# Attention scores as two row tiles of three products, with keys and queries kept in place

## The chip, the cores and the metric

The kernel runs on one core of one Trainium2 chip. The time is the device time of one execution in microseconds; the lower the better. A matmul here is one instruction of TensorE with its own weight load; VectorE, ScalarE and GpSimd each run their instructions in order, and SyncE (SP) issues all DMAs from one queue in order.

## The reference, cut to what matters

The program is a two-layer trunk over 1024 latent and 256 context tokens: differential attention, a dense MLP, an S5 mixer with a GLU, and a second MLP, with norms and gates between. Only the attention is touched by the change. There are 8 heads; each has two softmax maps over the same values:

```python
def attend(q, k, v):
    s = jnp.einsum('bqhcd,bkhcd->bhcqk', q, k).astype(jnp.float32)   # c = 2 maps, d = 64
    p = jax.nn.softmax(s, axis=-1)
    w = p[:, :, 0] - lam * p[:, :, 1]
    o = jnp.einsum('bhqk,bkhe->bqhe', w.astype(v.dtype), v)          # e = 128
    return rmsnorm(o, subln_g) * (1.0 - lambda_init)
```

Latent queries read all 1280 keys, context queries the 256 context keys. Queries and keys of latent tokens are rotated by their position before this. All operands are float32.

## The kernel before

**Precision.** A float32 operand x is kept as two fp32r numbers, hi (x rounded) and lo (x - hi). Most products are made as three: hi x hi, hi x lo and lo x hi (`mm3`, lines 130 to 134).

**Units.** The attention (`phase_b`, line 679) runs over 8 heads of 9 units each, 72 in all. Unit 0 holds two tiles of 128 context queries against 256 keys; units 1 to 8 hold one tile of 128 latent queries each against 1280 keys. Two units (1 and 2, 3 and 4, ...) are a pair of 256 queries. The instructions of the four compute engines are written in a fixed order by hand (`manual`, line 644); a framework puts in the waits between engines.

**One unit, in the order written** (loop at line 876):

- `scores` (568): both maps of the unit into PSUM. The two maps' 64 features have hi and lo stacked to 128 rows. For each map the keys are one array of [hi; lo], and the queries are there twice, as [hi; lo] and as [lo; hi], so that two products over 128 rows make all four terms. A unit of 1280 keys takes 8 products of 512 columns and 4 of 256. Map 0 fills columns 0 to 1280 of PSUM (banks 0, 1 and half of 2), map 1 columns 1280 to 2560 (the other half of bank 2, banks 3 and 4).
- `maxima` (584, L594): one VectorE pass per map copies scores out of PSUM and takes the row's minimum of the negated scores.
- `values` (713), in units where a pair is complete: 30 products of 256 columns of the weights `wT` with the values of the head, into bank 6.
- Three parts, each with transpositions of the *previous* unit's weights (`w_part`, L627: 4, 2 and 4 blocks of 128 keys), then a fill: some of the eight projection products (three matmuls each) of one group of the *next* head's keys or queries. The table AHEAD says which unit projects which group: units 0, 2, 5 and 7 have a group of 512 tokens, 1 and 3 one of 256, units 4, 6 and 8 none. FILLS says how the eight are cut over the parts, (0, 3, 6, 8) if nothing else is given.
- Part 0 is read out by ScalarE (hi, L635) and VectorE (lo, L636); parts 1 and 2 by a ScalarE copy (L640) and two GpSimd passes (L641, L642). Parts 0 and 2 of a unit with a group share bank 5; without a group part 2 uses bank 7, which the projections use otherwise. Part 1 uses half of bank 6.
- Between them stand, for this unit, the first exponential (`exps`, L604 on ScalarE) in part 0, and in part 1 the second exponential and `combine` (L612, L613, L615 on VectorE: w = p0 - factor x p1). In units with `values` of a latent pair ("late"), parts 0 and 1 are read out only behind `combine`.
- At the end: the pair's output (`pair_out`, L724, L725), its row sums one unit later (`pair_sums`, L731), and pieces of the projection's own tail (`next_post`): read-out (L528, L529, or L523, L524 for context), a swap of rows by four DMAs, a GpSimd product (L534), an addition (L537) and the hi/lo split (`split`, L137 on ScalarE and L138 on VectorE).

**Keys and queries by way of DRAM.** The split of a group goes into a staging buffer, and two DMAs store it to `Kd` or `Qd`. The next head's keys are loaded again as one array per map (`load_k`), the queries by three DMAs for each pair of tiles (`load_q`). The last of these loads are issued behind unit 8's scores.

**Beside it.** Unit 3 also holds three small VectorE instructions of the previous head's norm (L737 to L739); head 7 has no projections, but 60 products of the output projection in parts of six (`wo_group`).

Of the kernel before, what the change touches and what calls it, by code (L numbers as in the profile page):

```python
# [13 lines left out]
KB = 256  # L14
# [56 lines left out]
class Prog:  # L71
# [431 lines left out]
    def proj_group(self, h, T, g, wt):  # L503
# [7 lines left out]
        q, sw, qc, s = self.rq, self.rs, self.rc, self.stg[:, :, 0:n]  # L511
# [4 lines left out]
        def out():  # L516
            dst = self.Kd if T else self.Qd
            for c in range(2):
                self.dma(dst[h % 2, c, :, c0 : c0 + n].rearrange("(l r) n -> r l n", l=2),
                         s[64 * c : 64 * c + 64].bitcast(F32))  # L520

        def direct():
            nc.scalar.activation(s[:, 0], b, AF.Copy, scale=scale)  # L523
            nc.vector.scalar_tensor_tensor(s[:, 1], b, scale, s[:, 0].bitcast(F32), ALU.mult, ALU.subtract)  # L524
            out()
# [13 lines left out]
        def store():  # L539
            self.split(s[:, 0], s[:, 1], qc)  # L540
            out()
# [25 lines left out]

    def scores(self, u, Q, K):
        mm = self.nc.tensor.matmul
        if u == 0:  # L570
            for t in range(2):
                for c in range(2):
                    o = self.PS[:, 512 * t + 256 * c : 512 * t + 256 * c + 256]
                    for r in range(2):
                        mm(o, Q[:, c, r, 128 * t : 128 * t + 128], K[c][:, 0:256], start=r == 0, stop=r == 1)
            return
        qs = slice(128 * ((u - 1) % 2), 128 * ((u - 1) % 2) + 128)
        for c in range(2):
            for k0, k1 in (((0, 512), (512, 1024), (1024, 1280)), ((0, 256), (256, 768), (768, 1280)))[c]:
                for r in range(2):  # L580
                    mm(self.PS[:, 1280 * c + k0 : 1280 * c + k1], Q[:, c, r, qs], K[c][:, k0:k1], start=r == 0, stop=r == 1)  # L581


    def maxima(self, u, p, sm):
        ts = self.nc.vector.tensor_scalar
        if u == 0:
            for t in range(2):
                for c in range(2):
                    i = 512 * t + 256 * c
                    ts(p[c][:, 256 * t : 256 * t + 256], self.PS[:, i : i + 256], 1.0, None, ALU.mult, ALU.min,  # L590
                       accum_out=sm[:, 2 * t + c : 2 * t + c + 1])
        else:
            for c in range(2):
                ts(p[c], self.PS[:, 1280 * c : 1280 * c + 1280], 1.0, None, ALU.mult, ALU.min, accum_out=sm[:, c : c + 1])  # L594
# [21 lines left out]

    def w_part(self, u, w, n, tb):

        if u == 0:
            for kt in range(2):  # L620
                for t in range(2):
                    self.nc.tensor.transpose(tb[:, 256 * kt + 128 * t : 256 * kt + 128 * t + 128],
                                             w[:, 256 * t + 128 * kt : 256 * t + 128 * kt + 128], self.ident)
            return shaped(tb, (2, 256)), self.wT[0][:, 0:2], self.wT[1][:, 0:2]
# [1954 lines left out]
```

## Time and profile before

| | us |
|---|---|
| median of 3 runs | 2850.67 (2849.14 to 2854.11) |
| the profiled execution, its span | 2849.8 |
| head 0, first scores to the next head's | 222.7 to 293.5 |
| heads 1 to 6 | 293.5 to 763.5 |
| head 7 and what follows it in this stage | 763.5 to about 870 |

The profiled execution has no other time than its span; it lies within the three runs, and their median is 0.9 us above it. Rows of a timeline give the start in us from the span's start, the duration, engine, line, operation, what it writes and reads and its shape; brackets hold the idle time of the engine before it and what ended that. Rows of stretches give, for each engine, the time in which it was busy and its instructions. A duration on TensorE reaches to the end of the pipeline; how fast products follow each other is seen from their starts.

### The profile page before, as it was taken

The page shows a single profiled execution, that of the slowest core. Times are in us where ns is not written, and L with a number is a line of the kernel's source. Part 1 is how long each engine was busy: PE and PEld are TensorE (multiplying, and loading weights), DVE is VectorE, ACT ScalarE, POOL GpSimd, SP SyncE. Part 2 cuts the span into 40 slices and gives each one's busy share as a digit, 9 for nine tenths or more (in the row PEclk, how much of TensorE's full clock was granted, in tenths as well). Part 3 has the DMA queues.
Part 4 walks back from the last instruction along what each step waited for, and adds up shares of the span by engine and source line. Part 5 has one row for each costly group of instructions (what it writes and reads, how often), then busy time and mean ns, then how long its engine had stood idle before and what let it go on. Part 6 is the DMA issues. An engine that isn't in the chain of part 4 may idle for free.

```text
span 2849.8 us, 43385 instructions
## 1 busy us (share of the span) xinstructions
PE 2723.3 (96%) x15229; PEld 2283.1 (80%) x15229; DVE 2019.8 (71%) x2984; ACT 1369.5 (48%) x2583; POOL 1037.2 (36%) x901
## 2 busy tenths in 40 slices
PE   6999999999999999999999999789999999999999
PEld 4688888888877887778877878688887778888887
DVE  6357788888873667767698878799543597668466
ACT  3425555565653753333444445487444633344443
POOL 3314676766663600000030013688121143336414
PEclk9999999999999999999999999899999999999999
DMA  9955555655825359886799878579742144476544
GB/s 279 319 172 188 152 173 172 177 171 171 256 91 182 128 179 316 294 302 216 249 312 310 272 238 263 169 228 306 235 154 98 66 163 160 155 246 227 167 131 142
DMA packets 414823, 586.30 MB, mean 206 GB/s; under 512 B 41870, under 2 KB 260236, under 8 KB 411404
## 3 DMA queue, kind: packets, MB, share of 16 engines
q1 hardware_dynamic: 414604, 583.52, 63.5%
q8 instruction: 120, 1.97, 0.3%
q14 instruction: 99, 0.81, 0.1%
HBM read 396.38 MB, written 182.82 MB: 203 GB/s over the span
## 4 chain that ended last, share of the span: by engine, by line
PE 76%; DVE 9%; DMA 5%; issue 4%; POOL 3%; ACT 2%; SPq 1%; DVEq 0%; ACTq 0%; POOLq 0%
PE PS L132 21%; PE PS L134 20%; PE PS L133 20%; PE PS L581 4%; PE PS L627 2%; PE PS L1928 2%; PE PS L1963 2%; DMA FU<-in_mlp_w 1%; DMA Ta<-FU 1%; PE PS L202 1%; DVE R L138 1%; SPq L80 1%; DVE F L615 1%; ACT F L604 1%; DVE H L138 1%
## 5 line engine op out<-in xcount | busy, mean ns | idle before, releaser
L132 PE MATMUL PS<-H 128*128 128x512 f32 x1072 | 420.6, 393 | 2.7 <-ACT H L137 1.7
L134 PE MATMUL PS<-H 128*128 128x512 f32 x1072 | 417.5, 390 | 2.8 <-DVE H L138 1.5
L133 PE MATMUL PS<-H 128*128 128x512 f32 x1072 | 417.7, 390 | 0.0
L132 PE MATMUL PS<-H,R 128*128 128x512 f32 (+1 forms) x828 | 308.0, 374 | 4.3 <-ACT R L137 2.0
L133 PE MATMUL PS<-H,R 128*128 128x512 f32 (+1 forms) x828 | 298.6, 361 | 0.0
L134 PE MATMUL PS<-H,R 128*128 128x512 f32 (+1 forms) x828 | 298.0, 361 | 0.0
L132 PEld LDWEIGHTS PS<-H 128*128 128x128 f32 x1072 | 201.2, 188 | 50.5 <-issue 6.4
L134 PEld LDWEIGHTS PS<-H 128*128 128x128 f32 x1072 | 201.2, 188 | 46.1 <-DVE H L138 2.3
L133 PEld LDWEIGHTS PS<-H 128*128 128x128 f32 x1072 | 201.3, 188 | 40.6
L604 ACT ACTIVATE F<-F,stat 128x1280 f32<-128x1280 f32 x128 | 174.3, 1362 | 106.6 <-DVE F L594 106.5
L137 ACT ACTIVATE H<-U 128x640 fp32r<-128x640 f32 x216 | 131.9, 674 | 172.6 <-PE PS L133 138.3
L137 ACT ACTIVATE R<-W 128x512 fp32r<-128x512 f32 (+1 forms) x184 | 128.7, 707 | 174.1 <-PE PS L133 101.5
L132 PE MATMUL PS<-R,H 128*128 128x512 f32 x520 | 208.0, 401 | 3.3 <-ACT H L137 3.3
L134 PE MATMUL PS<-R,H 128*128 128x512 f32 x520 | 205.0, 396 | 1.8 <-DVE H L138 1.8
L133 PE MATMUL PS<-R,H 128*128 128x512 f32 x520 | 204.5, 394 | 0.0
L138 DVE TENSOR_TENSOR H<-U,H 128x640 fp32r<-128x640 f32 x216 | 165.1, 797 | 50.6 <-ACT H L137 49.6
L138 DVE TENSOR_TENSOR H<-W,H 128x512 fp32r<-128x512 f32 (+1 forms) x137 | 125.2, 924 | 102.8 <-ACT H L137 102.1
L594 DVE TENSOR_SCALAR_CACHE_REDUCE F<-PS 128x1280 f32<-128x1280 f32 x128 | 185.2, 1483 | 9.3 <-PE PS L581 9.1
L137 ACT ACTIVATE H<-W 128x512 fp32r<-128x512 f32 (+2 forms) x158 | 95.4, 613 | 188.7 <-PE PS L133 116.8
L132 PEld LDWEIGHTS PS<-H,R 128*128 128x128 f32 x828 | 157.6, 191 | 30.2 <-issue 4.1
L134 PEld LDWEIGHTS PS<-H,R 128*128 128x128 f32 x828 | 157.0, 190 | 25.2 <-issue 0.8
L641 POOL TENSOR_SCALAR R<-F 128x256 fp32r<-128x256 f32 (+1 forms) x128 | 126.5, 989 | 136.0 <-ACT F L640 122.4
(534 smaller groups left out, 6860.0 us busy)
## 6 DMA issues: line engine op xcount, KB each, us to landing
W<-in_mlp_w SPq DMA_DIRECT2D x176, 256.0 KB
U<-Aa SPq DMA_DIRECT2D x108, 320.0 KB
Aa<-FU SPq DMA_DIRECT2D x91, 320.0 KB
Ad<-F SPq DMA_DIRECT2D x112, 256.0 KB
W<-Ad SPq DMA_DIRECT2D x112, 256.0 KB
FU<-in_mlp_w SPq DMA_DIRECT2D x32, 512.0 KB
Ta<-FU SPq DMA_DIRECT2D x16, 1024.0 KB
U<-in_ada_w SPq DMA_DIRECT2D x32, 512.0 KB
```

The costliest lines, as they stand in the source:

```text
L132: mm(out, ah, bh, start=first, stop=False, **kw)
L133: mm(out, ah, bl, start=False, stop=False, **kw)
L134: mm(out, al, bh, start=False, stop=last, **kw)
L137: self.nc.scalar.activation(hi, src, AF.Copy)
L138: (lo_eng or self.nc.vector).tensor_tensor(lo, src, hi.bitcast(F32), ALU.subtract)
L581: mm(self.PS[:, 1280 * c + k0 : 1280 * c + k1], Q[:, c, r, qs], K[c][:, k0:k1], start=r == 0, stop=r == 1)
L594: ts(p[c], self.PS[:, 1280 * c : 1280 * c + 1280], 1.0, None, ALU.mult, ALU.min, accum_out=sm[:, c : c + 1])
L604: nc.scalar.activation(p[c], p[c], AF.Exp, bias=sm[:, c : c + 1], scale=-1.0, accum_out=sn[:, 0:1] if c else s0[:, u + 1 : u + 2])
L627: self.nc.tensor.transpose(tb[:, 128 * (kt - k0) : 128 * (kt - k0) + 128], w[:, 128 * kt : 128 * kt + 128], self.ident)
L641: nc.gpsimd.tensor_scalar(hi, t, 1.0, 0.0, ALU.mult, ALU.add)
L1928: mm(b[:, o : o + 160], X[:, d, i, 64 * j : 64 * j + 128], U[:, 4 * n + i, cols], start=True, stop=True)
L1963: mm(o, cs[d][n % 2][j][:, i], W[:, d, i], start=False, stop=d == 1 and j == 1)
```

## The change

1. **Scores.** Hi and lo are no longer stacked. Keys and queries are each two arrays, hi and lo, of 128 rows: map 0 in rows 0 to 63, map 1 in rows 64 to 127. For each chunk of keys there are three products (hi x hi, hi x lo, lo x hi) for each map, over 64 rows, the two maps in turn. Map 0 and map 1 use different rows of TensorE and different PSUM banks: map 0 columns 0 to 1280, map 1 columns 1536 to 2816. The term lo x lo is no longer computed. A unit of 1280 keys has 18 products in place of 12.
2. **In place.** For heads 1 to 7 the split writes keys and queries straight into the arrays that the scores read: two sets of keys, for even and odd heads, and one set of queries. Only head 0 still goes by way of `Kd` and `Qd`. The buffer R1 grows by 5 KB per partition to hold this.
3. **Banks of the transpositions.** In units with a group, part 0 goes to the unused halves of banks 2 and 5, as part 2 does in all units; part 0 of a unit without a group goes to bank 7.
4. **Order.** The first fill stands before part 0, the second before part 2, the third behind it. With the new FILLS the third is empty but in unit 1. The first exponential and the pair's sums stand ahead of part 0, the pair's output ahead of `combine`.

```diff
-    FILLS = {1: (0, 0, 4, 8), 3: (0, 4, 8, 8)}
+    FILLS = {0: (0, 4, 8, 8), 1: (0, 0, 4, 8), 2: (0, 3, 8, 8), 3: (0, 7, 8, 8)}
...
-        q, sw, qc, s = self.rq, self.rs, self.rc, self.stg[:, :, 0:n]
+        q, sw, qc = self.rq, self.rs, self.rc
+        hi, lo = (self.stg[:, j, 0:n] for j in range(2)) if h == 0 else self.operand(h, T, g)
...
         def store():
-            self.split(s[:, 0], s[:, 1], qc)
+            self.split(hi, lo, qc)
             out()
...
     def scores(self, u, Q, K):
...
+        if u == 0:
+            todo = [(256 * t, 256, 0, 128 * t) for t in range(2)]
+        else:
+            todo = [(k0, n, k0, 128 * ((u - 1) % 2)) for k0, n in ((0, 512), (512, 512), (1024, 256))]
+        for o, n, k0, q0 in todo:
+            for i, (x, y) in enumerate(((0, 0), (0, 1), (1, 0))):
                 for c in range(2):
...
+                    r = slice(64 * c, 64 * c + 64)
+                    self.nc.tensor.matmul(self.PS[:, 1536 * c + o : 1536 * c + o + n], Q[x][r, q0 : q0 + 128],
+                                          K[y][r, k0 : k0 + n], start=i == 0, stop=i == 2)
...
+    def part_bank(self, i):
+        b = self.PS
+        if i == 7:
+            return bass.AP(b.tensor, b.offset + 512 * 7, [list(b.ap[0]), [256, 2], [1, 256]])
+        return bass.AP(b.tensor, b.offset + 1280, [list(b.ap[0]), [1536, 2], [1, 256]])
...
-        Kr = Ring([self.view(self.R1, 5 * i, (1280,)) for i in range(3)])
...
+        Ks = [[self.view(self.R1, 10 * i + 5 * j, (1280,)) for j in range(2)] for i in range(2)]
...
+        qhi = self.view(self.R1, 20, (1280,))
+        Qs = [[qhi[:, 256:768], qhi[:, 768:1280], qhi[:, 0:256]], [self.rv(12, 512), self.rv(14, 512), self.rv(56, 256)]]
...
-                    a = self.FILLS.get(u, (0, 3, 6, 8))
+                    a = self.FILLS.get(u, (0, 4, 8, 8))
...
+                def part(i):
+                    if i < parts:
+                        tb = pb[:, 256:512] if i == 1 else self.part_bank(7 if i == 0 and not groups else 2)
+                        ready.append((*self.w_part(prev[1], prev[2], i, tb), i == 0))
+
                 if pv:
                     values(*pv)
...
+                fill(0)
+                if front:
+                    self.exps(u, 0, p, sm, s0, sn)
...
+                while sums and sums[0][0] <= n:
+                    sums.pop(0)[1]()
+                part(0)
+                if not late:
                     next_post()
+                    evac()
+                part(1)
+                if late:
+                    next_post()
+                if front:
+                    self.exps(u, 1, p, sm, s0, sn)
                 if pv:
                     pair_out(*pv)
...
+                    self.combine(u, p, s0, sn)
+                evac()
+                fill(1)
+                part(2)
+                evac()
+                fill(2)
+                if front and u == 0:
+                    next_post()
                 next_post()
```

More of the change, by code (lines that the diff above doesn't have):

```diff
@@ L894, in phase_b @@
                         load_v(h + 1)
[L895 to L897 removed]
                     if h < 7:
                         groups = [self.proj_group(h + 1, *a, wts[a[0]]) for a in (self.AHEAD[u],)] if u in self.AHEAD else []
[L900 to L904 removed]
+                    self.scores(u, queries(pair), Ks[h % 2])
                     self.maxima(u, p, sm)
```

133 lines of the change are left out of this document (47 added, 86 removed).

## The prediction

> **What bounds the kernel now.** I read the page's span and its chain of waits first, then the table by stretch for one attention head, then who waited for whom from 300 to 760 us, then the timelines of three engines through that head.
>
> ```profile
> span 2849.8 us, 43385 instructions
> ...
> PE 76%; DVE 9%; DMA 5%; issue 4%; POOL 3%; ACT 2%; SPq 1%; DVEq 0%; ACTq 0%; POOLq 0%
> ```
>
> ```profile
> 528.59:558.89 30.30, 27.93 (x175) 24.59 (x174) 24.58 (x44) 17.86 (x42) 19.10 (x20) 1.00 0.80 239
> 558.89:583.52 24.63, 23.43 (x155) 20.75 (x153) 20.92 (x33) 14.85 (x28) 18.23 (x18) 1.00 0.52 148
> 583.52:606.93 23.41, 23.41 (x157) 21.21 (x155) 20.14 (x27) 14.07 (x26) 15.98 (x15) 1.00 0.37 104
> sum 78.34, PE 74.77 PEld 66.56 DVE 65.64 ACT 46.78 POOL 53.32; mean PE 24.92 PEld 22.19 DVE 21.88 ACT 15.59 POOL 17.77
> ```
>
> ```profile
> DVE stat L612 <- ACT F L604: 50.4, 41, 2.0
> ```
>
> The three stretches are head 4: units 0 to 2, 3 to 5, 6 to 8. TensorE looks like the bound, 74.77 of 78.34 us. But VectorE has 65.64 us of work, and much of its idle time cannot be filled: its largest wait is for an exponential, 1.2 us at a time. Each unit has a loop through the engines: scores (TensorE), two row minima (L594, VectorE), two exponentials (L604, ScalarE), the combination (L612, L613, L615, VectorE). VectorE works in order, so the next unit's minima stand behind this unit's combination. Its rows in units 3 to 5:
>
> ```profile
> 558.85 1.09 DVE L138 TENSOR_TENSOR R<-FC,R 128x512 fp32r<-128x512 f32 x1
> 560.05 0.69 DVE L529 SCALAR_TENSOR_TENSOR FC<-PS,W 128x512 f32<-128x512 f32 x1
> 560.66 1.48 DVE L594 TENSOR_SCALAR_CACHE_REDUCE F<-PS 128x1280 f32<-128x1280 f32 x1
> ...
> 562.06 1.49 DVE L594 TENSOR_SCALAR_CACHE_REDUCE F<-PS 128x1280 f32<-128x1280 f32 x1
> ...
> 565.44 0.16 DVE L612 RECIPROCAL stat<-stat 128x1 f32<-128x1 f32 x1 [1.28 <-ACT F L604]
> ...
> 569.26 1.48 DVE L594 TENSOR_SCALAR_CACHE_REDUCE F<-PS 128x1280 f32<-128x1280 f32 x1
> ...
> 573.68 0.16 DVE L612 RECIPROCAL stat<-stat 128x1 f32<-128x1 f32 x1 [0.92 <-ACT F L604]
> ...
> 577.23 1.48 DVE L594 TENSOR_SCALAR_CACHE_REDUCE F<-PS 128x1280 f32<-128x1280 f32 x1
> ...
> 581.85 0.16 DVE L612 RECIPROCAL stat<-stat 128x1 f32<-128x1 f32 x1 [1.12 <-ACT F L604]
> ...
> 585.20 1.49 DVE L594 TENSOR_SCALAR_CACHE_REDUCE F<-PS 128x1280 f32<-128x1280 f32 x1 [0.18 <-PE PS L581]
> ```
>
> From 560.66 to 581.85 the three bracketed waits are VectorE's only long ones: no minimum there waits for TensorE. The scores are ready before VectorE comes to them; only at 585.20 does it wait for them. TensorE in that stretch:
>
> ```profile
> 556.62 0.60 PE L627 MATMUL PS<-ident,F 128*128 128x128 f32 x4
> ...
> 558.89 2.49 PE L581 MATMUL PS<-R,R 128*128 128x512 f32 x12
> 561.22 0.60 PE L627 MATMUL PS<-ident,F 128*128 128x128 f32 x4
> ...
> 572.57 2.57 PE L581 MATMUL PS<-R,R 128*128 128x512 f32 x12
> 576.34 0.66 PE L627 MATMUL PS<-ident,F 128*128 128x128 f32 x4 [1.20 <-DVE R L636]
> ```
>
> Unit 5's transpositions begin 3.77 us after its scores, which take 2.33 us (558.89 to 561.22): they wait for the bank that L636 still reads, behind unit 4's combination. So from unit 3 to unit 5 the loop through VectorE sets the time; in units 1, 2, 6 and 8, with their long runs of products, it is TensorE.
>
> **The change part by part.** *Scores.* The nearest rows to row tiles are plain products of 256 columns, and the way into and out of column tiles of 128x32:
>
> ```profile
> 508.06 0.28 PE L133 MATMUL PS<-R 128*128 128x256 f32 x1
> 508.18 0.28 PE L134 MATMUL PS<-R,R 128*128 128x256 f32 x1
> ```
>
> ```profile
> 1068.06 0.39 PE L134 MATMUL PS<-H,R 128*128 128x512 f32 x1
> 1068.38 0.64 PE L202 MATMUL PS<-FU,scT 128*32 128x256 f32 x8
> 1068.94 0.50 PE L132 MATMUL PS<-H,R 128*128 128x512 f32 x1
> 1069.28 0.39 PE L133 MATMUL PS<-H,R 128*128 128x512 f32 x1
> 1069.51 0.39 PE L134 MATMUL PS<-H,R 128*128 128x512 f32 x1
> ```
>
> Products of 512 columns follow each other every 0.23 us, those of 256 every 0.12. Today's eight and four are 8 x 0.23 + 4 x 0.12 = 2.32 us a unit, the 2.33 seen. The new form is 18 products, nine pairs. If the two of a pair run side by side that is 6 x 0.23 + 3 x 0.12 = 1.74 us; if one after the other, 3.48. No row of this trace has row tiles. But eight column-tile products of 256 fit in 0.56 us, entry and exit included; one after the other they would be 0.96. Tiles do overlap there, and I take 1.74. The visit has a price: the first tile starts 0.32 us after a product that is usually followed after 0.23, and the first full product after it holds the next up for 0.34 in place of 0.23. From 1068.06 to 1069.28 are 1.22 us; less two products of 0.23 that leaves 0.76 for eight tile products in two rounds, at least 0.24 of work, so a visit costs at most 0.52 us and at least the 0.20 of its two ends. I take 0.40, since the first of these wider weight loads has no cover either. A unit's scores become 2.14 us, 0.19 less; unit 0's six pairs of 256 become 0.72 + 0.40 = 1.12 in place of 0.96. Per head 8 x 0.19 - 0.16 = 1.4 us less on TensorE. If the two weight loads of a pair don't overlap, a 256 pair costs up to 0.24, and that is 8 x 3 x 0.12 + 6 x 0.12 = 3.6 us a head more.
>
> The Trainium skill (TensorE: Matmul & The Clock Gate, section "Measured speedup vs the span model") gives 3.07x for four row tiles, not 4x, and no row here shows it. An estimate from that page: a pair would cost 1.3 times 0.23 or 0.12, a unit's scores 2.26 + 0.40 = 2.66 us, and eight heads would carry some 33 us more on TensorE: up to 2901 by the page, 2868 by the rows.
>
> *Fills ahead of transpositions.* Four projection products of 512 columns are 12 x 0.23 = 2.76 us. They now stand ahead of the first four transpositions, whose bank in units with a group is now the rest of banks 2 and 5, beside scores. The dependency goes by banks: the minimum at 585.20 is over the first map alone, and yet waited for a later product in the bank it shares with the second. So these transpositions wait for both minima, where today (561.22) they start right behind the scores. The fill covers that wait on TensorE; without this cover it would be the minima's 2.9 us. It does not cover what is queued behind the transpositions on ScalarE:
>
> ```profile
> 557.26 0.60 ACT L640 ACTIVATE F<-PS 128x512 f32<-128x512 f32 x1 [0.49 <-PE PS L627]
> ...
> 558.07 0.65 ACT L137 ACTIVATE R<-FC 128x512 fp32r<-128x512 f32 x1
> ...
> 561.85 0.60 ACT L635 ACTIVATE R<-PS 128x512 fp32r<-128x512 f32 x1 [1.65 <-PE PS L627]
> ...
> 563.96 1.36 ACT L604 ACTIVATE F<-F,stat 128x1280 f32<-128x1280 f32 x1
> ```
>
> L635 stands ahead of the second exponential in both orders. Today it is over long before, and that exponential starts 0.4 us after the second minimum's end (562.06 + 1.49 to 563.96). After: the transpositions and their latency 0.63 (561.22 to 561.85), L635 0.5, then the exponential: 1.2 us. So the combination of units 3, 5 and 7 comes 0.8 us later after its minima.
>
> *Where the third transpositions go.* Unit 2's fills were 3, 3 and 2 products; they become 3, 5, 0, and its last four transpositions end the unit. Behind them on ScalarE are L640 and the key store's split L137, behind that on VectorE L138, then L529, then unit 3's minima. Today they start 2.27 us before the scores at 558.89 (556.62); then 0.44 (0.60 less the last one's tail). L640 would start at 559.09, L137 at 559.6, L138 at 560.3 in place of 558.85, L529 at 561.4, the first minimum at 562.0 in place of 560.66. (With the maps interleaved the first is complete only with the second, at 558.89 + 2.14 + 0.28 = 561.3: hidden behind it.) L529 also frees bank 7 for unit 3's fill, which waits for it from 561.0 to 562.0.
>
> *The loop, summed.* Against unit 3's start: minima +1.35, second exponential +0.8, L612 at 567.6 in place of 565.44, +2.15. The rows to 577.23 follow each other without slack, so unit 5's minima are +2.15 too; its order adds 0.85, and L612 stands at +3.0. Unit 5's minima are over at 582.3; then 0.44 + 0.22 of transpositions, a fill of 2.76 and 0.44 again: 586.2 in place of 583.52, **+2.65 us**. Units 6, 8, 1 and 2, which TensorE sets, give back 4 x 0.19 = 0.76; unit 7 has unit 5's order and loses about 0.8. Per head +2.7.
>
> *Keys and queries in place.* This takes 12 stores and 19 loads a head out of SP's queue. The wait they caused is in unit 0:
>
> ```profile
> 531.24 0.97 PE L575 MATMUL PS<-R,R 128*128 128x256 f32 x6 [2.17 <-DMA R<-Kd]
> 532.41 0.66 PE L627 MATMUL PS<-ident,F 128*128 128x128 f32 x4 [0.19 <-DVE R L636]
> ```
>
> The 2.17 us go, but the transpositions behind still waited for L636 after them; in the new order the fill takes that place, and bank 7, which it writes, is what unit 8's L636 reads. I count nothing; bounds: nothing, and 2.17 us a head. The splits on ScalarE and VectorE are as many as before. The pair's output (L724, L725 on GpSimd, its store on SP) moves up a step in its queues; only the sums a unit later wait for it: nothing.
>
> **Sum.** Heads 1 to 6: 6 x 2.7 = 16.2. Head 0 has no norm work between units 3 and 4, so more slack: half, 1.4. Head 7 has no projections: 0. Together +17.6 on the profiled span of 2849.8, 2867.4; the median of the runs is 0.9 above that span: **2868 us**.
>
> **Rivals.** *TensorE sets the time and the change is faster.* For it: 76% of the chain, and 3.57 us of TensorE idle a head (78.34 - 74.77). Then 1.4 and the idle go: 7 x 5.0 = 35 us, 2816; with half of it 2833. Against it: three minima in a row that never waited for scores. It decides if unit 3's L612 comes no later after its scores than today. *The row tiles run one after the other.* Then 3.48 + 0.40 a unit, +1.55, and 0.9 in unit 0, 13.3 a head; TensorE is the bound again and the idle hides 3.6: 9.7 x 8 = 78, about 2929. For it: no row tile in the trace; against it: the column tiles. *Nothing measurable:* the 1.4 on TensorE and most of the DMA wait balance the loop's 2.7, 2850.
>
> **Chances.** Slower by the loop 0.52, serial tiles 0.10, faster 0.30, balanced 0.08. About 0.2% (5.7 us) is what a measurement of this kernel tells from no change. So slower 0.62, same 0.08, faster 0.30. The range leaves out the serial tiles and the far end of the fast case, and reaches up to a loop case whose weight loads don't overlap (3.6 a head, partly hidden): 2822 to 2890; the loop case alone is 2856 to 2890.
>
> **What would show it.** Right: 18 products of scores a unit in about 2.1 us; L635 right before the second exponential in units 3, 5 and 7; L636 waiting for L635; the stretch of units 3 to 5 near 27.3 us; fills that wait for L529 or L636. Wrong: units 3 to 5 shorter than 24.63 us, minima that wait for TensorE in every unit, or scores above 3 us.

## The result and the profile after

The changed kernel takes **2898.2 us** (median of four runs, 2893.9 to 2901.0) where the kernel before takes 2850.7 beside it: a ratio of 1.0158, 95% interval 1.0143 to 1.0172. The forecast of slower was right, its size was not: 47.5 us in place of 17.6, and above the range's upper end of 2890.

Line numbers have moved: the scores are L577 now, the minima L590, the exponentials L600, the combination L608, L609 and L611, the transpositions L631, their direct read-out L642 (ScalarE) and L643 (VectorE), their raw copy L647 with GpSimd's L648 and L649, the sums and their read-out L742 and L743.

First, where the time is. The table by stretch (us, then each engine's busy time, granted clock, DMA share, GB/s) for head 0, heads 1 to 6, and head 7 to its last scores, of the kernel before:

```profile
222.71:293.53 70.82, 69.84 (x431) 62.22 (x431) 53.98 (x86) 41.33 (x79) 35.77 (x34) 0.98 0.51 161
293.53:763.53 470.00, 449.67 (x2877) 400.30 (x2875) 390.17 (x605) 278.93 (x566) 314.37 (x301) 1.00 0.61 180
763.53:843.40 79.87, 71.83 (x398) 60.16 (x397) 58.84 (x93) 44.18 (x88) 52.17 (x55) 0.94 0.45 142
```

and of the changed one:

```profile
218.11:298.17 80.06, 72.17 (x483) 60.45 (x482) 54.69 (x89) 42.53 (x81) 37.43 (x34) 0.98 0.31 98
298.17:805.87 507.70, 467.19 (x3187) 395.61 (x3186) 371.80 (x603) 282.48 (x566) 318.07 (x300) 0.99 0.29 89
805.87:890.75 84.88, 69.44 (x442) 55.80 (x442) 58.07 (x94) 44.35 (x89) 53.23 (x55) 0.94 0.29 89
```

Heads 1 to 6 lose 37.7 us, 6.3 a head, head 0 loses 9.2 and head 7 5.0. That is 51.9, while the two profiled executions differ by 42.3 (2892.1 against 2849.8): ahead of head 0's scores and behind head 7's last the changed one is 4.6 and 5.0 us shorter. That is not shown to be a gain of the change: the first scores start anywhere from 216.3 to 222.4 us in the row-tile runs below (runs 1, 6 and 7), whose code ahead of them is the same. The DMA engines carry half as much; what that is worth is seen in experiment 7. Head 4 by the same three stretches as in the prediction (units 0 to 2, 3 to 5, 6 to 8):

```profile
552.39:584.05 31.66, 29.91 (x190) 25.31 (x189) 22.22 (x42) 16.13 (x38) 17.70 (x18) 0.95 0.42 127
584.05:612.40 28.35, 24.54 (x173) 20.48 (x172) 20.72 (x33) 15.50 (x29) 19.05 (x19) 1.00 0.15 44
612.40:638.07 25.67, 24.27 (x174) 20.79 (x173) 19.48 (x29) 15.88 (x30) 17.08 (x16) 1.00 0.22 60
```

The middle stretch grew by 3.7 us (24.63 to 28.35; 27.3 was predicted). But the outer ones grew too, by 1.4 and 2.3 us, where the prediction had a gain of 0.4 in the first and a loss of 0.4 in the last. So something costs outside units 3 to 5 too. Who waited for whom, from 300 to 780 us (total, times, longest):

```profile
DVE R L643 <- ACT R L642: 33.6, 21, 2.8
...
PE PS L577 <- ACT F L647: 26.4, 44, 1.3
...
DVE F L590 <- PE PS L577: 18.5, 16, 1.5
```

The second row is new: TensorE's *scores* wait for ScalarE's raw copy of the transpositions. Over the whole run the page has 39.4 us of it:

```profile
L577 PE MATMUL PS<-R 64*128 64x512 f32 (+1 forms) x832 | 157.8, 376 | 40.6 <-ACT F L647 39.4
```

The last row goes with it: minima that wait for the scores, 18.5 us, which the kernel before had for 2.1 (experiment 1 shows that it follows). The timeline of TensorE through units 3 and 4 of head 4:

```profile
583.52 0.60 PE L631 MATMUL PS<-ident,F 128*128 128x128 f32 x4
584.05 0.50 PE L577 MATMUL PS<-R 64*128 64x512 f32 x1
584.80 0.72 PE L577 MATMUL PS<-R 64*128 64x512 f32 x3 [0.26 <-ACT F L647]
...
589.85 0.39 PE L134 MATMUL PS<-H,R 128*128 128x256 f32 x1 [1.06 <-POOL R L138]
...
601.40 0.50 PE L577 MATMUL PS<-R 64*128 64x512 f32 x1
603.16 0.72 PE L577 MATMUL PS<-R 64*128 64x512 f32 x3 [1.26 <-ACT F L647]
```

The third transpositions end a unit, and the next unit's first product runs at once: it is of the first map, in bank 0. The second product, of the second map in bank 3, waits. The transpositions lie in halves of banks 2 and 5, so nobody reads bank 3. But one read-out takes both halves in one access, from column 1280 to column 3072, and bank 3 lies between them. Second, in unit 3 a product of the fill, 589.85, waits 1.06 us for GpSimd's L138. ScalarE, VectorE and GpSimd in that unit:

```profile
591.82 0.60 ACT L642 ACTIVATE R<-PS 128x512 fp32r<-128x512 f32 x1 [0.32 <-PE PS L631]
592.31 1.36 ACT L600 ACTIVATE F<-F,stat 128x1280 f32<-128x1280 f32 x1
...
586.71 1.49 DVE L590 TENSOR_SCALAR_CACHE_REDUCE F<-PS 128x1280 f32<-128x1280 f32 x1
...
588.12 1.49 DVE L590 TENSOR_SCALAR_CACHE_REDUCE F<-PS 128x1280 f32<-128x1280 f32 x1
...
592.45 0.69 DVE L643 TENSOR_TENSOR R<-PS,R 128x512 fp32r<-128x512 f32 x1 [2.83 <-ACT R L642]
593.79 0.16 DVE L608 RECIPROCAL stat<-stat 128x1 f32<-128x1 f32 x1 [0.65 <-ACT F L600]
...
588.51 1.29 POOL L138 TENSOR_TENSOR R<-W,R 128x512 fp32r<-128x512 f32 x1
```

The second minimum is over at 589.6, its exponential starts at 592.31, right behind L642, as predicted; but L642 waits for a fill of seven products, and the fifth of them waits for L138, which writes the second half of the query weights until 589.8.

### The profile page after: what moved, and what is told of

It reads as the page before. It is cut to its first block, busy times and chain, and to the rows that moved or that the text cites. A ratio compares the mean times of both kernels' runs of the same rounds, so it can differ in the third digit from the quotient of the medians.

```text
span 2892.1 us, 43801 instructions
## 1 busy us (share of the span) xinstructions
PE 2739.7 (95%) x15645; PEld 2272.2 (79%) x15645; DVE 2002.1 (69%) x2984; ACT 1374.6 (48%) x2583; POOL 1041.5 (36%) x901
## 4 chain that ended last, share of the span: by engine, by line
PE 70%; DVE 9%; issue 6%; POOL 6%; DMA 5%; ACT 4%; SPq 1%; POOLq 0%; DVEq 0%; ACTq 0%
PE PS L132 20%; PE PS L134 19%; PE PS L133 19%; PE PS L1937 2%; PE PS L577 2%; PE PS L1972 2%; PE PS L631 1%; ACT F L600 1%; PE PS L202 1%; POOL R L649 1%; SPq L80 1%; DVE R L138 1%; ACT F L647 1%; DVE H L138 1%; DMA W<-in_mlp_w 1%
## 5 line engine op out<-in xcount | busy, mean ns | idle before, releaser
L132 PE MATMUL PS<-H 128*128 128x512 f32 x1072 | 420.5, 393 | 2.6 <-ACT H L137 1.7
L134 PE MATMUL PS<-H 128*128 128x512 f32 x1072 | 417.5, 390 | 2.8 <-DVE H L138 1.5
L132 PE MATMUL PS<-H,R 128*128 128x512 f32 (+1 forms) x828 | 307.0, 373 | 3.5 <-ACT R L137 2.0
L134 PE MATMUL PS<-H,R 128*128 128x512 f32 (+1 forms) x828 | 299.9, 363 | 6.0 <-POOL R L138 6.0
L600 ACT ACTIVATE F<-F,stat 128x1280 f32<-128x1280 f32 x128 | 174.6, 1364 | 185.0 <-DVE F L590 184.9
L132 PEld LDWEIGHTS PS<-H 128*128 128x128 f32 x1072 | 201.1, 188 | 50.6 <-issue 6.2
L134 PEld LDWEIGHTS PS<-H 128*128 128x128 f32 x1072 | 201.2, 188 | 46.2 <-DVE H L138 2.4
L137 ACT ACTIVATE H<-U 128x640 fp32r<-128x640 f32 x216 | 131.9, 675 | 170.5 <-PE PS L133 144.8
L137 ACT ACTIVATE R<-W 128x512 fp32r<-128x512 f32 (+1 forms) x184 | 128.9, 708 | 175.8 <-PE PS L133 100.0
L132 PE MATMUL PS<-R,H 128*128 128x512 f32 x520 | 207.5, 400 | 4.0 <-ACT H L137 3.3
L590 DVE TENSOR_SCALAR_CACHE_REDUCE F<-PS 128x1280 f32<-128x1280 f32 x128 | 185.5, 1486 | 34.6 <-PE PS L577 34.5
L134 PE MATMUL PS<-R,H 128*128 128x512 f32 x520 | 205.5, 396 | 2.0 <-DVE H L138 2.0
L138 DVE TENSOR_TENSOR H<-U,H 128x640 fp32r<-128x640 f32 x216 | 164.8, 798 | 50.5 <-ACT H L137 48.6
L577 PE MATMUL PS<-R 64*128 64x512 f32 (+1 forms) x832 | 157.8, 376 | 40.6 <-ACT F L647 39.4
L138 DVE TENSOR_TENSOR H<-W,H 128x512 fp32r<-128x512 f32 (+1 forms) x137 | 124.8, 921 | 102.9 <-ACT H L137 102.3
L132 PEld LDWEIGHTS PS<-H,R 128*128 128x128 f32 x828 | 158.2, 191 | 35.4 <-issue 4.1
L137 ACT ACTIVATE H<-W 128x512 fp32r<-128x512 f32 (+2 forms) x158 | 95.5, 614 | 186.2 <-PE PS L133 117.4
L134 PEld LDWEIGHTS PS<-H,R 128*128 128x128 f32 x828 | 158.5, 191 | 32.5 <-POOL R L138 7.4
```

Source lines behind the costliest of these rows:

```text
L132: mm(out, ah, bh, start=first, stop=False, **kw)
L134: mm(out, al, bh, start=False, stop=last, **kw)
L137: self.nc.scalar.activation(hi, src, AF.Copy)
L138: (lo_eng or self.nc.vector).tensor_tensor(lo, src, hi.bitcast(F32), ALU.subtract)
L577: self.nc.tensor.matmul(self.PS[:, 1536 * c + o : 1536 * c + o + n], Q[x][r, q0 : q0 + 128], K[y][r, k0 : k0 + n], start=i == 0, stop=i == 2)
L590: ts(p[c], self.PS[:, 1536 * c : 1536 * c + 1280], 1.0, None, ALU.mult, ALU.min, accum_out=sm[:, c : c + 1])
```

## The experiments

The theory after the traces: three waits of the new order and its banks make the loss, (A) the scores behind L647, (B) the second exponential behind the fill, (C) the fill behind the weights' split. The rival for each: what it frees is lost at the next wait. All times are medians; the kernel before, run beside each, has 2850 to 2854, and the ratios are to it.

**1. Halves side by side.** The second map's scores move to columns 1792 to 3072 with their short product first, so the two half banks are one piece, 1280 to 1792. Unit 0's second map moves to column 2048 with it; nothing else is changed.

```
-  ((0, 512), (512, 512), (1024, 256)), second map at 1536 + k0
+  ((0, 256, 512), (512, 768, 512), (1024, 0, 256)), second map at 1792 + k1
-  [list(b.ap[0]), [1536, 2], [1, 256]]
+  [list(b.ap[0]), [256, 2], [1, 256]]
```

> The changed kernel with the second map's scores laid from column 1792 on, its short product first, so that the two half banks of the first and third transpositions lie side by side (columns 1280 to 1792) and their read-out L647 touches no column from the one half to the other. Same number of instructions. Theory A (the read-out over columns 1280 to 3072 is held to touch everything between its halves, so the second map's first scores wait for it; 39.4 us of idle TensorE ahead of L577, and they are on the path): that idle falls under 10 us and the time falls by 20 to 40 us, to 2858 to 2878. Rival (the scores are not what ends last; the loop through VectorE and ScalarE sets the time and the idle only moves behind the scores): the wait goes, the time stays within 8 us of 2898.

Measured: 2879.6 us (ratio 1.0097, 1.0073 to 1.0122), 18.5 less than the changed kernel. TensorE's waits from 300 to 780 us, where L578 are the scores and L648 the raw copy:

```profile
PE PS L132 <- DVE R L644: 14.7, 17, 1.1
...
PE PS L578 <- ACT F L648: 2.5, 6, 0.4
```

26.4 us of waiting became 2.5 (5.8 of 39.4 over the whole run), and the minima wait 4.2 us for scores in place of 18.5. So the one read-out did hold up the bank that lies between its halves, and the wait was on the path, though only half of its 39.4 us: theory A holds, its gain just short of the 20 to 40 us. The waits between engines are put in by the framework, so this is likely its rule for such an access; no run separates it from the chip's. With this wait gone the scores can be read. TensorE's timeline from unit 6 into unit 7:

```profile
601.71 1.25 PE L632 MATMUL PS<-ident,F 128*128 128x128 f32 x10
602.89 0.74 PE L578 MATMUL PS<-R 64*128 64x512 f32 x4
...
604.65 0.28 PE L578 MATMUL PS<-R,R 64*128 64x256 f32 x2
605.64 0.50 PE L132 MATMUL PS<-H,R 128*128 128x512 f32 x1 [0.71 <-DVE R L644]
```

The 18 products take 1.76 us from the first start to the last pair's, 1.88 with that pair.

**2. The maps in turn,** to see whether two row tiles run side by side: all nine products of the first map, then the second's nine, on the halves side by side.

```
-  for o, n, k0, q0 in todo: for i, (x, y) in ...: for c in range(2):
+  for c in range(2): for o, n, k0, q0 in todo: for i, (x, y) in ...:
```

> Joined halves with all nine products of the first map ahead of the nine of the second, so that no two products of different row tiles alternate. Theory (in the changed kernel two row tiles run side by side, a pair of 512 columns every 0.23 us): the products come one every 0.23 or 0.12 us, a unit's scores take 3.5 to 3.9 us in place of some 2.0, and the time rises by 40 to 110 us, to 2920 to 2990. Rival (the two products of a pair run one after the other in any order): scores and time unchanged, 2875 to 2885.

Measured: 2907.8 us (two runs), 28 more than run 1; 40 to 110 was expected. The scores there:

```profile
603.63 0.72 PE L578 MATMUL PS<-R 64*128 64x512 f32 x2
...
606.75 0.28 PE L578 MATMUL PS<-R,R 64*128 64x256 f32 x1
```

3.12 us from the first start to the last, in place of 1.76: the row tiles do run side by side, and the rival of serial tiles is out. Of the 1.36 us more a unit (64 units of this shape, 87 us of TensorE) only 28 reach the end. Which units pass it on is seen in units 3 to 5 and 6 to 8 of head 4, run 1 first, then this one:

```profile
567.89:596.10 28.21, 23.93 (x174) 19.77 (x173) 20.72 (x33) 15.36 (x29) 19.02 (x19) 1.00 0.15 44
596.10:620.82 24.72, 23.07 (x173) 20.03 (x172) 20.51 (x30) 15.81 (x30) 16.92 (x16) 1.00 0.23 61
```

```profile
585.81:614.22 28.41, 26.91 (x172) 23.00 (x171) 20.75 (x33) 15.54 (x29) 19.02 (x19) 1.00 0.15 43
614.22:640.87 26.65, 26.65 (x173) 23.21 (x172) 20.52 (x30) 15.70 (x30) 15.99 (x16) 1.00 0.22 65
```

Of some 4.1 us more of scores, units 3 to 5 pass on 0.2 and units 6 to 8 1.9; units 0 to 2 pass on 1.6 (30.30 in place of 28.70). So in units 3 to 5 TensorE's own work is not what ends last, as the prediction had it, and a shorter score stage can be worth little there; in the others about half of it counts.

**3. The two parts apart.** The old order on row tiles, and the new order on the kernel before.

```
e3:  row tiles, banks, keys in place; loop and FILLS of the kernel before
e4:  kernel before; loop and FILLS of the changed one (bank 5 for the transpositions)
```

> Row tiles, their banks and the keys and queries in place as in the changed kernel, but the order and the fills of the kernel before (transpositions ahead of the fills). Theory (the two belong together: transpositions beside the scores wait for both minima, and without the fill nothing covers that wait, some 2.5 us in each of the five units with a projection group): slower than the changed kernel, 2930 to 2990. Rival (the new order is what costs; row tiles and banks by themselves save): 2835 to 2855.

> The kernel before (scores stacked over 128 rows, transpositions in bank 5 by themselves, keys and queries through memory) with the new order and the new fills alone. Theory (the order by itself makes the loop longer: second exponential behind L642 behind the fill, unit 2's third transpositions at the unit's end): slower than the kernel before by 15 to 35 us, 2866 to 2886. Rival (the order costs nothing where transpositions have a bank of their own; the loss comes from the scores' wait for the shared banks): 2845 to 2857.

Measured: 3010.3 us with the old order (ratio 1.056), 2877.5 with the new order alone (1.009, 1.0066 to 1.0115). Both theories hold, the first beyond its range. Row tiles whose transpositions share banks with scores need the fills ahead: in the old order these transpositions wait 41.1 us for the minima L590, from 300 to 780 us. The new order by itself costs 27 us. The stretch of units 3 to 5 of its head 4:

```profile
573.54:601.67 28.13, 24.59 (x157) 20.95 (x155) 21.05 (x33) 15.34 (x29) 19.37 (x19) 1.00 0.45 130
```

It is 3.5 us longer than before (28.13 against 24.63). So the loss is 27 for the order and, with run 1, 18.5 for the split halves; row tiles with joined halves add 2 to the order's loss, which is no more than the intervals.

**4. The exponential ahead of L642** in units 0, 2, 3, 5 and 7.

```
                 next_post()
+                if front: self.exps(u, 1, p, sm, s0, sn)
                 evac()
```

> The changed kernel with the second exponential ahead of the read-out L642 on ScalarE in units 0, 2, 3, 5 and 7 (the others have that order already). Theory B (the second exponential waits behind L642, and this behind a fill of 4 or 7 products and four transpositions, so VectorE's combination is late): the second exponential starts some 0.4 us behind the second minimum in units 3 and 5 (in unit 3 at about +6 us from the unit's first scores in place of +8.3), the stretch of units 3 to 5 falls from 28.4 to 25 to 26.5 us, the time by 12 to 25 us, to 2873 to 2886. Rival (the scores' wait for L647, or TensorE's own work, ends last in these units too): the exponential moves, the time stays within 6 us of 2898.

Measured: 2914.7 us, 16 more. ScalarE and VectorE in unit 3 of that run:

```profile
600.99 0.17 ACT L743 ACTIVATE FC<-PS 128x2 f32<-128x2 f32 x1 [2.06 <-PE PS L742]
601.05 1.35 ACT L600 ACTIVATE F<-F,stat 128x1280 f32<-128x1280 f32 x1
...
603.02 0.69 DVE L643 TENSOR_TENSOR R<-PS,R 128x512 fp32r<-128x512 f32 x1 [4.17 <-ACT R L642]
```

The exponential still stood behind L743, which reads sums that TensorE makes behind the fill; and VectorE's L643, which stands ahead of the combination, now waited for an L642 behind the exponential. So this run did not test B. Moving it past both does:

**5. Both exponentials first,** in every unit, VectorE's subtraction behind the combination; on joined halves with the fills of experiment 6, and the same without row tiles.

```
  exps(u, 0)
+ exps(u, 1)          # ahead of the sums and of L643
...
  combine(...)
+ subtraction (L644)  # was ahead of the combination
```

> Row tiles with the joined halves and both edits of the fills; in every unit both exponentials stand on ScalarE right behind each other, ahead of the sums' read-out and of the first transpositions' read-out L643, and VectorE's subtraction L644 stands behind the combination. Theory B again, in full (the second exponential waits behind a fill, by the sums' read-out and by L643; in the earlier trial it was moved past L643 alone, still stood behind the sums' read-out and VectorE's L643 there waited for it): the second exponential starts 0.4 us behind the second minimum's end in every unit, unit 3's combination 2 us earlier, the time 10 to 25 us less than the 2870 of the run with both fills, 2845 to 2860. Rival (the bank that the subtraction frees is free later, so the third transpositions and the fills wait for it): the combination moves, the time does not fall, 2865 to 2890.

> The same order on the scores of the kernel before (stacked, no row tiles, transpositions in bank 5, keys and queries through memory). Theory (row tiles, banks and keys in place are worth nothing measurable): within 5 us of the run with row tiles beside it. Rival (with the exponentials out of the way TensorE ends last and the row tiles' 1.4 us a head show): slower than that run by 6 to 12 us.

Measured: 2929.9 and 2919.0 us, slower than every other form of the new order. The second exponential does start where theory B wants it (in unit 3 of head 4 at 601.01, the second minimum ends at 600.97), and the time is 60 us above the run with both fills (2869.8, experiment 6): as a gain, theory B falls. TensorE's waits in the first of them (L962 is the subtraction, L744 the sums' read-out):

```profile
PE PS L632 <- DVE R L962: 18.3, 14, 1.9
PE PS L632 <- ACT FC L744: 17.9, 21, 1.1
PE PS L132 <- DVE R L962: 16.1, 16, 2.0
```

TensorE waits 52 us there for reads that free its banks. As a way to a faster kernel the early exponential is out; since the subtraction moved with it, what it would bring by itself was not measured. That the later release of the transposition banks weighs more is what these waits suggest. Without row tiles it was 11 us faster, against both expectations; that difference was not followed.

**6. The fills of units 2 and 3,** on joined halves: unit 3 four products ahead of the transpositions in place of seven, unit 2 again 3, 3 and 2, and both.

```
-  2: (0, 3, 8, 8), 3: (0, 7, 8, 8)
+  e5: 3: (0, 4, 8, 8)    e6: 2: (0, 3, 6, 8)    e7: both
```

> Joined halves, and unit 3's fill ahead of the transpositions cut from 7 products to 4 as in the kernel before (0, 4, 8, 8). Theory C (in unit 3 the fifth product waits 1.03 us for GpSimd's L138, the split of the second half of the query weights, and the transpositions, L643 and the second exponential stand behind it; three products of 0.36 stand there too): the second exponential starts about 2 us earlier after unit 3's scores, unit 3 falls from 9.7 us to 7.5 to 8.2, the time by 10 to 17 us against the joined halves, to 2862 to 2870. Rival (what unit 3 loses units 4 and 5 give back, since their loop through VectorE sets the time): unit 3 is shorter, the time within 5 us of 2880.

> Joined halves, and unit 2's fills again 3, 3 and 2 products, so that its third transpositions stand two products (1.4 us) ahead of the unit's end, as in the kernel before. Theory D (as predicted: the third transpositions at the end hold L648, L137, L138, L529, and with them unit 3's minima and its fill, which waits 0.80 us for L529): unit 3's first minimum starts about 1.8 us after its scores in place of 2.9, the wait for L529 falls under 0.3 us, the time falls by 4 to 8 us against the joined halves, to 2872 to 2876. Rival (unit 3's fill then waits for the weights' split as long as it does now, 1.03 us and the 0.8 more): within 3 us of 2880.

> Both edits of the fills of units 2 and 3 on the joined halves. If theories C and D hold and add up: 2855 to 2864, the stretch of units 3 to 5 under 26 us. If the loop gives back what they free: above 2868.

Measured: 2867.7 us (ratio 1.0052, 1.0035 to 1.0069), 2880.7 and 2869.8, against 2879.6 of run 1. Unit 3's fill is worth 12 us, as theory C had it. Unit 3 of the first of the three, from scores to scores, has 8.08 us (from 566.25 to 574.33) in place of 9.7, and L138 is no longer among what TensorE waits for:

```profile
566.25 0.73 PE L578 MATMUL PS<-R 64*128 64x512 f32 x4
...
574.33 0.73 PE L578 MATMUL PS<-R 64*128 64x512 f32 x4
```

Unit 2's split alone is worth nothing: the fill starts earlier and waits longer for the same weights, 8.7 us at L134 for L138 in place of 5.6:

```profile
PE PS L134 <- POOL R L138: 8.7, 6, 1.5
```

So the rival won there, and the prediction's step of unit 2's third transpositions was no loss by itself: the weights came last. Both together, above the 2855 to 2864 that adding up would give, gain 0.4 us a head more in heads 2 to 6 and lose it in head 1, whose unit 0 has an odd row, below.

**7. The subtraction that holds bank 7.** In units 1, 4, 6 and 8 the first transpositions' subtraction stands behind the combination, and the next unit's fill waits for it (the first row of run 1's waits). Three ways to end that, all on top of both fills: GpSimd splits them; they change banks with the third transpositions; VectorE subtracts ahead of the combination's long step.

```
e8:   direct read-out: i == 0   ->   i == 0 and not late
e9:   bank 7 where no group: part 0   ->   part 2
e10:  combine: reciprocal, factor, [subtraction], long step
```

> The same as the run with both edits of the fills, and in the units with values products (1, 4, 6, 8) the first transpositions are read by ScalarE into a raw tile and split by GpSimd, as the other two parts are, so that VectorE has no L644 behind its combination there and bank 7 is free as soon as ScalarE has read it. Theory E (in units 4, 6 and 8 VectorE's own loop, minima, exponential, combination and L644, sets the time, and the fills of units 0, 5 and 7 wait some 0.7 to 1.1 us for that L644): 0.6 us less in three to four units and most of these waits, 10 to 20 us less than the run with both edits, 2838 to 2853. Rival (GpSimd's 1.9 us more in each of these units holds back the raw tiles or the values products, or TensorE ends last there): within 4 us of the run with both edits, or slower.

> The run with both edits of the fills, and in the units without a projection group the first transpositions go into the joined halves and the third into bank 7 (as in the kernel before), in place of the other way round. Theory F (the fills of units 0, 5 and 7 wait 0.9 to 1.3 us for VectorE's L644 only because it reads bank 7; a third part there is read by ScalarE early): TensorE's wait of L132 for L644, some 17 us from 300 to 780 us, goes, and the time falls by 8 to 15 us, to 2855 to 2862. Rival (L644 then holds the halves that the next unit's last score products write, so the scores and the minima wait for it): the wait moves to the scores' line, the time is equal or higher, 2868 to 2885.

> The run with both edits of the fills, and in units 1, 4, 6 and 8 ScalarE reads the first transpositions ahead of the pair's output and VectorE subtracts (L644's operation) ahead of the long third step of the combination in place of behind it: the same instructions, bank 7 is free 1.5 to 2 us earlier. Theory F (the fills of units 0, 5 and 7 wait for that subtraction): their wait falls from 0.9 to 1.3 us to under 0.3, the time falls by 8 to 15 us, to 2855 to 2862; head 1's unit 0, where the idle of 3 us is followed by 13 products at 0.43 us in place of 0.23, falls from 13.8 us to about 9.5. Rival (the combination ends later and with it the minima and the exponentials of the next unit, so the loop takes it back): within 4 us of the run with both edits, 2870.

Measured: 2889.8, 2868.9 and **2859.0** us (ratio of the last 1.0028, 1.0015 to 1.004), against 2869.8. GpSimd's extra work pushes its rotation L534 back, and VectorE's L537 waits for that, 52.2 us in place of 25.9:

```profile
DVE FC L537 <- POOL FC L534: 52.2, 11, 6.2
```

With the banks changed, the scores wait for the subtraction in place of the fill (16.8 us), as the rival said:

```profile
PE PS L578 <- DVE R L644: 16.8, 12, 1.7
```

Subtracting first is worth 10.8 us by these medians and some 8 by the ratios (1.0055 to 1.0028). From 300 to 780 us TensorE's L132 no longer waits for the subtraction (17.5 us before), but in the profiled executions heads 2 to 6 do not get shorter (79.5 and 79.8 us): there the loop takes it back, as the rival said. Head 1 is some 3.7 us shorter and head 7 3.0, head 0 is 1.9 longer; in head 1 the half pace of the last section is gone. So not all of the 10.8 is shown to come from the wait. Two more kernels went with it: the head before's norm moved behind the third transpositions, and the same order and edits without row tiles.

```
e11:  e10 with norm_pair behind part(2); evac()
e13:  kernel before + new order + the fills and the subtraction of e10
```

> The same as the run with the subtraction first, and the norm of a pair of the head before (L776 on VectorE, the splits on ScalarE and GpSimd) is issued behind the read-out of the third transpositions in place of ahead of the combination, so that on GpSimd its 2 us stand behind L649 and L650 of that part. Theory G (the values products of units 1, 4 and 8 wait 0.3 to 1.1 us for GpSimd's L650, which stands behind this norm): that wait goes, the time falls by 4 to 9 us more, to 2846 to 2858. Rival (GpSimd's next piece, the split L138 of stored keys or the rotation L534, is late in its place): within 4 us of the run before it, or slower.

> The new order alone on the kernel before (scores stacked, no row tiles, keys and queries through memory) with the same three edits as the run with the subtraction first: fills of unit 2 and unit 3, subtraction ahead of the long step of the combination. It stands beside that run (2859 us) with everything equal but row tiles, banks and keys and queries in place. Theory (as predicted, row tiles save 0.19 us a unit on TensorE, and keys and queries in place nothing, so some 1.4 us a head where TensorE sets the time): slower than that run by 4 to 12 us, 2863 to 2871. Rival (the loop through VectorE sets the time and hides all of it): 2855 to 2862. Other rival (row tiles cost by the banks that transpositions share with them): under 2852.

Measured: 2880.7 us for the first, 22 slower: GpSimd's L652 (L650 in the runs above) is hardly waited for by TensorE any more (1.3 us in place of 10.1), but ScalarE's half of the split, L137, is late now and VectorE's L138 waits 15.3 us for it (0.3 before); that this makes the 22 is likely, not shown. The second is 2858.7 (1.0017, 1.0007 to 1.0027), where the same edits with row tiles and keys in place have 2859.0. In one order and with the worst waits gone, row tiles, their banks and keys and queries in place are together worth nothing that can be measured; the three were not taken apart.

**8. The same subtraction in the kernel before.**

```
  v.scalar_tensor_tensor(sn[:, 3:4], ...)
+ subtraction of the first transpositions (L636's operation), units 1, 4, 6, 8
  v.scalar_tensor_tensor(p[0][:, k], ...)
```

> The kernel before with one edit, VectorE's subtraction (L636's operation) in units 1, 4, 6 and 8 ahead of the long third step of the combination in place of behind it. Theory (unit 5's transpositions wait 1.2 us for that subtraction in the kernel before, and unit 0's 0.2): the wait falls under 0.3 us, and the time by 4 to 10 us, to 2840 to 2846. Rival (the combination ends 0.7 us later and unit 5's and unit 7's minima with it, which wait for VectorE): within 4 us of 2850, or slower.

Measured: 2858.8 us (1.0026, 1.0014 to 1.0038), slower. TensorE's transpositions wait for the combination itself (L617) as long as they waited for the subtraction (11.6 us before):

```profile
PE PS L629 <- DVE F L617: 11.4, 11, 2.1
```

So in the kernel before it is VectorE's chain that sets unit 5, and not the place of the subtraction in it. No kernel here beats the one before.

## Why the prediction was right, and where it was wrong

**Direction and mechanism of the order: right.** In units 3 to 5 the loop through VectorE decides, and not TensorE: 4.1 us more of scores there change their stretch by 0.2 (experiment 2). The new order makes that loop longer: 27.3 us were predicted for the stretch, 28.35 measured, 28.13 with the order alone. L642 stands right ahead of the second exponential, and L643 waits 33.6 us for L642, as listed. That the sum came so near is in part luck. With the order alone unit 3 of head 4 is 3.1 us longer (9.73 in place of 6.66), and a wait that the sum did not have is in it, below; unit 5 is 0.1 longer (11.08, 10.95), where some 0.5 was put, and unit 7 0.2 shorter (9.27, 9.49), where a loss of 0.8 was put.

**Row tiles: right on TensorE.** In run 1 unit 6 goes from 596.10 to 602.89, 6.8 us, against 7.0 before (583.52 to 590.53); 0.19 less was worked out. What it is worth was put too high: units 1, 2, 6 and 8 were to give back 0.76 us a head, but a head of run 1 is 0.2 us longer than one of the order alone. The Trainium skill (TensorE: Matmul & The Clock Gate, section "Measured speedup vs the span model") gives 3.07x for four row tiles, and the estimate from it was 2901. The time came near it, but not for that reason: two tiles here do nine pairs in 1.88 us, where the full doubling is the 1.74 of the prediction; the first pair, which holds the next up for 0.35 us in place of 0.23, makes most of the rest. The page's discount for four does not show with two.

**The step that failed** is the one on the third transpositions: "L640 would start at 559.09", behind the next unit's first scores. It priced what stands behind that read-out on ScalarE and VectorE, but not what TensorE has next to write: the next unit's scores were taken to start at once and to end at 561.3, both maps. In fact the second map's first product waits for that read-out, 44 times from 300 to 780 us: 39.4 us of idle TensorE in the run. Without it the time is 18.5 us less, and the attention of the profiled executions 24.6 (experiment 1). Some 5 us of this is half clock: behind that wait heads 2 to 4 take 85.7 us where heads 5 and 6 take 83.9 (last section). For head 4's first stretch this is the whole loss: with joined halves it has 28.70 us, less than the 30.30 before. For its last stretch it is 1.0 of 2.3; the order alone is 1.2 longer there (24.63), where 0.4 was put. The step "the dependency goes by banks" was too narrow as well: one read of two half banks held the bank between them too.

**Terms that were mis-sized.** In unit 3 the minima were put at +1.35 us and are at +0.9 (586.71, 2.66 behind the scores; 560.66 was 1.77 behind). L612, now L608, was put at +2.15 and is at +3.2 (9.74 in place of 6.55). So from the minima to L608 2.3 us were lost where 0.8 was put. The wait of 1.06 us for L138 is most of the difference: the weights' split was not among the things a longer fill could wait for, though it stands on GpSimd's queue in every head. Cutting the fill is worth 12 us (6). The reason given for unit 2, third transpositions at its end, cost nothing by itself. The fill's wait for bank 7 was seen ("is what unit 8's L636 reads") and counted as nothing; it is 14.7 us of TensorE's waits in run 1, and ending it is worth at most 11 (7). **Heads 0 and 7** were put at 1.4 and nothing and have 9.2 and 5.0; joined halves alone take 4.5 and 1.4 of that (80.06 to 75.5, and 84.88 to 83.5), since the wait for L647 needs no projections. **Keys and queries in place:** nothing, as said; the DMA traffic halved, and with the row tiles no time came of it.

By the ratios the 1.58% of the loss fall to 0.97 with joined halves, 0.55 with both fills as well and 0.28 with the subtraction first: some 17, 12 and 8 us, each at the size that it had at that point, and some 8 that remain and were not taken apart. The heads in the middle show the same with less noise, from one head's first scores to the next's, in the one profiled execution of each kernel:

| kernel | median of heads 2 to 6, us |
|---|---|
| before | 78.3 |
| changed | 85.7 (83.9 at full clock) |
| joined halves (1) | 81.6 |
| new order alone (3) | 81.5 |
| joined halves and unit 3's fill (6) | 80.0 |
| and unit 2's (6) | 79.5 |
| and the subtraction first (7) | 79.8 |
| the same without row tiles (7) | 79.4 |

The order by itself costs 3.1 us a head, where 2.7 were predicted for the whole change; the split halves come on top.

## What to carry to other kernels

When a change moves a read-out, ask what every engine does next with the *memory* it holds, the engine that fills it above all, and not only what stands behind the read-out in its queue. A read of two separate pieces in one access can hold all that lies between them; put the pieces side by side. An engine that is busy 95% of the time can still have little to win: lengthen its work in one run and see how much of it reaches the end, and in which stretch.

## What the runs showed that was not expected

In places TensorE ran at half pace for some microseconds behind a wait. In the run with both fills, head 1, unit 0 (stretch, busy times, granted clock in the third column from the right):

```profile
300.58:305.87 5.29, 5.29 (x13) 4.13 (x13) 2.01 (x9) 1.20 (x4) 3.53 (x4) 0.50 0.00 0
```

```profile
300.58 0.79 PE L132 MATMUL PS<-H,R 128*128 128x512 f32 x1 [2.89 <-DVE R L644]
```

The first twelve products from there take 5.29 us, one every 0.43 but for the first, in place of 0.23, and the clock granted is 0.50: a wait of 2.9 us cost some 2.5 us more behind it. The Trainium skill (TensorE: Matmul & The Clock Gate, section "What's actually happening") puts half the clock behind an idle window of about 3.4 us. The half pace agrees; the idle before it was shorter here.

How long TensorE idled does not decide it in these traces. In the kernel before, the idle of 2.17 us at 531.24 left the clock at 1.00. In the changed kernel unit 0 of heads 2 to 6 waits 1.28 us for L647; in heads 2, 3 and 4 the half pace follows, in heads 5 and 6 it does not (head 4, then head 5):

```profile
554.02 0.50 PE L577 MATMUL PS<-R 64*128 64x256 f32 x3 [1.28 <-ACT F L647]
...
556.13 0.63 PE L134 MATMUL PS<-H,R 128*128 128x512 f32 x1
556.55 0.63 PE L132 MATMUL PS<-H,R 128*128 128x512 f32 x1
```

```profile
639.69 0.50 PE L577 MATMUL PS<-R 64*128 64x256 f32 x3 [1.28 <-ACT F L647]
...
641.35 0.40 PE L134 MATMUL PS<-H,R 128*128 128x512 f32 x1
641.59 0.40 PE L132 MATMUL PS<-H,R 128*128 128x512 f32 x1
```

The granted clock of the 5.5 us from 554.00 is 0.69, and of the 5.5 us from 639.70 it is 1.00. What decides stays open here.
